# A streaming trunk of conv and attention on one core: coarser places at which attention's steps enter the projections

## The chip, the cores and the metric

The kernel runs on one core of a Trainium2 chip. The metric is the device time of one execution in microseconds (us). The kernel before takes 1231.87 us, the median of 3 runs (1231.71 to 1232.19).

The engines go by the names that the profile uses: PE is TensorE's matrix unit and PEld its weight loads, DVE is VectorE, ACT is ScalarE, POOL is GpSimd, SP is SyncE (it only issues DMAs here).

## The reference, cut to what matters

Two layers, each a SwiGLU feed-forward, a token mixer and a second SwiGLU feed-forward; layer 0 mixes by a short gated convolution, layer 1 by attention with a forget gate. There are 256 prompt frames and 64 frames of a running stream (which attends also to 256 cached frames), 320 frames in all; model width 1024, 16 heads of 64, all in float32. The part that the change touches is layer 1's mixer:

```python
def fox_project(xn, w_in, b_f, gq, gk):
    proj = xn @ w_in
    q, k, v = ...                       # 1024 columns each, 16 heads of 64
    f_logit = proj[..., 3 * D_MODEL:] + b_f
    q = rms_norm(q, gq)                 # per head
    k = rms_norm(k, gk)
    logf = jax.nn.log_sigmoid(f_logit)
    return q, k, v, logf

def fox_attend(q, k, v, c_q, c_k, q_pos, k_pos):
    s = jnp.einsum('bqhd,bkhd->bhqk', q, k) * (HEAD_DIM ** -0.5)
    decay = c_q - c_k                   # cumulative log forget, per head
    s = jnp.where(k_pos <= q_pos, s + decay, NEG_INF)
    p = jax.nn.softmax(s, axis=-1)
    return jnp.einsum('bhqk,bkhd->bqhd', p, v)

x = x + fox_attend(...) @ w_out         # prompt, and sample with its cache
```

Normalised keys, the values and the log forget gates of the new frames are outputs too.

## The kernel before, in words

**Whole program.** Seven stages follow one another: two feed-forwards around the conv mixer, the first feed-forward of layer 1, attention, the last feed-forward, with PE busy nearly all the time. Weights come in slabs, at most three at a time, each by two DMA loads on SP's queue. Every float32 weight is split into a high part (ACT casts it, L133) and a low part (DVE subtracts, L136), so that a product is three matmuls in a reduced float32 format (`mm3`, L153 to L158; high by high, high by low, low by high).

**Attention (L580 to L954).** PE's order there is not the order of the code but is made by a planner when the program is built (the loop at the end of `attn_mixer`, L927 to L954). It takes two kinds of work:

- *Dense work*, a generator, `dense()` (L878): the forget logits `pf`; then for each of two halves (eight heads) the projections of queries `pq`, keys `pk` and values `pv`, each by `project` (L847); then output projection `pm`. `project` takes its weights as two slabs, each half of the contraction (four of the eight 128-row pieces `k`), and computes three PSUM tiles `c`: two of 128 prompt frames (three matmuls for each `k`), and one for the 64 sample frames, high and low parts side by side (two matmuls for each `k`). Tiles go in the order 0, 1, 2 with the first slab and 2, 0, 1 with the second. A tile that has its second half is handed to `done`: `raw_tile` (ACT copies it out, squares it, DVE sums per head), or `value_tile`.
- *Side tasks*, a list: `gates` (L599: forget gates), `decay_tile` (per pair of heads, the mask rows: three loads per head from a DRAM copy on SP's queue, POOL adds the causal mask), `past` (loads of cached keys and values), `pair` (L746), `values_ready` (L838). There are eight pairs of heads, 0 to 3 in the first half.

A pair has four steps on PE: the *key step* (transposes of cached keys `kps` and of queries and keys `np`, from where DVE and ACT fill `ka` and `qa`, L755 to L765); the *scores* `sc` (five matmuls, L792, then `softmax`, L774 to L780, on DVE and ACT); the *transposes* `tk`, `tks` of the probabilities (L807; ACT copies them out, L810 and L813); the *output step* `oT` (L825, L830; cast to high and low by ACT L833 and DVE L834). Output projection needs a pair's result from all eight pairs; its first four tiles run over the pairs as they come.

Before each piece of dense work that `dense()` yields, the planner runs every side task whose due time has come by its own clock. That clock advances by the assumed cost of each piece, 0.2265 us (`MM`) for a projection matmul. The table `LAT` says how much later than its step a task is asked again: `norm` after the key projection (pairs 0, 2, 4, 6; two more for the odd ones), `evac` after a key step, `soft` for a softmax (counted from the end of the previous softmax where that is later), `vr` from the last value tile to the point from which a half's output steps may come. The other engines run in the order in which the code of these steps is reached, so a step that PE gets later also stands later on DVE, ACT, POOL and SP.

**Buffers.** There are four PSUM buffers for projections (`ps_mm`) and four for everything else in attention (`ps_aux`, taken by `aux(...)`): a key step takes three, scores three, transposes three, an output step one. One SBUF buffer, with the tag `ktok`, serves in turn the normalised key rows on the way out (POOL L726, then a store on SP's queue) and the 64 rows that are moved across partitions when the two halves of the sample tile are added up: `fold` (L682), a DMA on ACT's queue (L686), for queries and keys followed by DVE's add (L704), for values by POOL's. ACT issues such a DMA itself and stands until the buffer is free.

Of the kernel before, what the change touches and what calls it, by code (L numbers as in the profile page):

```python
# [30 lines left out]
KC = 8  # L31
# [3 lines left out]
SEGS = ((0, S), (S, TS))  # L35

PRE = 4
LAT = dict(rstd=2.5, gates=16, norm=8, evac=3.5, soft=5.5, pt=1, vr=1.5, out=1.8)


QT = 5
# [10 lines left out]
def trunk_kernel(  # L52
# [89 lines left out]
    def next_slab():  # L142
        if ready:
            return ready.pop(0)
        w, nk, load, split = open_slab()
        for k0 in range(0, nk, nk // 2):
            ks = slice(k0, k0 + nk // 2)
            load(ks)
            for part in split:
                part(ks)  # L150
        return w
# [428 lines left out]
    def attn_mixer(next_gain, pool):  # L580
# [9 lines left out]
        for b in range(2):  # L590
            pt = pool.tile([P, 9 * P], F32, tag=f"pt{b}", name=f"pt{b}")
# [7 lines left out]
        def gates(pf):  # L599
# [5 lines left out]
            st["RT"] = RT  # L605
            yield 0.4, LAT["rstd"]
            STT(r2T, RT, 1.0 / HD, RT, ALU.mult, ALU.mult)
# [27 lines left out]
            nc.gpsimd.dma_start(out=f_sample[0, 0], in_=lf[P - TS:P, 2])  # L635
            yield 0.8, LAT["gates"]

# [108 lines left out]
        def pair(p, n, vtok):  # L746
# [9 lines left out]
            for nj, g in zip(n, (gq, gk)):  # L756
# [5 lines left out]
                else:  # L762
                    by_tile = np_[:, :T].rearrange("p (i q) -> p i q", q=TS)
                    nc.scalar.activation(qa[b][0:HD, :, 0], by_tile[0:HD], AF.Copy, scale=g[0:HD])
                    TSC(qa[b][HD:P, :, 1], by_tile[HD:P], g[HD:P], None, ALU.mult)  # L765
            yield 0.85, LAT["evac"]
            while p not in st["rows"]:
# [14 lines left out]
        def attend(p, vpast, vtok):  # L782
# [14 lines left out]
            st["scored"][p] = 2  # L797
            st["soft"] = max(st["now"] + 1.65, st["soft"]) + LAT["soft"]
            yield 1.65, st["soft"] - st["now"] - 1.65

            kt = []
            for name, cols, heads_first in (("k0", (0, P, 2 * P, 4 * P), True), ("k1", (3 * P, 5 * P), True),
# [11 lines left out]
                kt.append(t)  # L814
            yield 1.0, LAT["pt"]
            while p not in st["v"]:
# [17 lines left out]
            TT(out=yl[:, p], in0=oT[:, :T], in1=yh[:, p].bitcast(F32), op=ALU.subtract)  # L834
            yield 1.5, LAT["out"]
            st["done"][p] = 6
# [8 lines left out]
        MM = 0.2265  # L845

        def project(name, done):  # L847


            pcs = {}  # L850
            for s in range(2):
                wh, wl = next_slab()
                wh, wl = (w.rearrange("p k c -> p (k c)").rearrange("p (k c) -> p k c", c=HW) for w in (wh, wl))
                for c in ((0, 1, 2), (2, 0, 1))[s]:
                    if s == 0:
                        pcs[c] = ps_mm.tile([P, 512], F32, tag="mm", name=name)
                    pc = pcs[c]
                    for kk in range(KC // 2):
                        k = s * (KC // 2) + kk
                        first, last = k == 0, k == KD - 1  # L860
                        if c == 2:
                            if not first:
                                nc.tensor.matmul(pc[0:TS], lhsT=xs[:, k, 0], rhs=wl[:, kk], start=False, stop=False)
                            nc.tensor.matmul(pc, lhsT=xs[:, k].rearrange("p a b -> p (a b)"), rhs=wh[:, kk],
                                             start=first, stop=last)
                            if first:
                                nc.tensor.matmul(pc[0:TS], lhsT=xs[:, k, 0], rhs=wl[:, kk], start=False, stop=False)
                            yield 2 * MM
                        else:
                            f = slice(c * P, (c + 1) * P)  # L870
                            nc.tensor.matmul(pc, lhsT=xh[:, k, f], rhs=wh[:, kk], start=first, stop=False)
                            nc.tensor.matmul(pc, lhsT=xl[:, k, f], rhs=wh[:, kk], start=False, stop=False)
                            nc.tensor.matmul(pc, lhsT=xh[:, k, f], rhs=wl[:, kk], start=False, stop=last)
                            yield 3 * MM
                    if s == 1:
                        done(c, pc)

        def dense():  # L878
            w = next_slab()
# [9 lines left out]
            for half in range(2):  # L889
                for j, name in enumerate(("pq", "pk")):  # L890
                    st["n"][j] = pool.tile([P, 3, HW], F32, tag=f"n{j}", name=f"n{j}_{half}")
                    st["m"][j] = pool.tile([P, 3, H // 2], F32, tag="qm", name=f"m{j}_{half}", bufs=2)
                    nc.gpsimd.memset(st["m"][j][TS:P, 2], 1.0)
                    yield from project(name, lambda c, pc: raw_tile(j, half, c, pc))
                    normalise(j, half)
                st["vtok"] = pool.tile([P, 3, HW], F32, tag="vtok", name=f"vtok{half}")
                for p in range(4 * half, 4 * half + 4):
                    side.append([pair(p, tuple(st["n"]), st["vtok"]), st["now"] + LAT["norm"] + 2.0 * (p % 2)])
                yield from project("pv", lambda c, pc: value_tile(half, c, pc))
                side.append([values_ready(half), 0.0])  # L900
# [63 lines left out]
    with tc.tile_pool(name="am", bufs=1) as pool:  # L964
        attn_mixer(g_ffn(1, 1), pool)
# [35 lines left out]
```

## Time and profile before

One execution was profiled; it took 1232.79 us, and the profiler's span of it is 1231.0 us.

| stretch of the span | what runs on PE | length, us | PE busy, us |
|---|---|---|---|
| 0 to 821.9 | feed-forwards and conv mixer | 821.90 | 820.75 |
| 821.9 to 928.2 | attention: logits, both halves' queries and keys, first values | 106.30 | 102.69 |
| 928.2 to 974.8 | attention: second values, first part of output projection | 46.60 | 45.92 |
| 974.8 to 992.6 | rest of output projection | 17.80 | 17.80 |
| 992.6 to 1231.0 | last feed-forward | 238.40 | 234.08 |

Instructions are named in the profile by line, engine, operation and tile (`out<-in`); L792 is line 792 of the kernel printed above. Matmuls overlap one another, so the length of one row is longer than its share of PE's time; the distance from start to start is what counts. A wait is put down to the producer that came last.

### The profile page before, as it was taken

How to read it: one execution, taken by the hardware profiler on the slowest of the kernel's cores; microseconds unless marked ns; L12 is line 12 of the kernel's file. 1: busy time of each engine (PE TensorE's matmuls, PEld its weight loads, DVE VectorE, ACT ScalarE, POOL GpSimd, SP SyncE). 2: the span in 40 equal slices, each digit the busy share in tenths (PEclk: the TensorE clock that was granted, in tenths of full speed). 3: DMA queues.
4: the chain of work that ended last, by engine and by line, in shares of the span. 5: the costliest groups of instructions: out<-in, count | busy, mean ns of one | idle time of the engine just before them, and what ended most of it. 6: DMA issues, size and time to landing. Idle time of an engine off the chain costs nothing.

```text
span 1231.0 us, 20252 instructions
## 1 busy us (share of the span) xinstructions
PE 1221.2 (99%) x8229; PEld 1188.5 (97%) x8229; DVE 764.4 (62%) x1322; ACT 493.0 (40%) x759; POOL 41.2 (3%) x95
## 2 busy tenths in 40 slices
PE   9999999999999999999999999999999999999998
PEld 9999999999999999999999999997778999999998
DVE  7665655586686655554856555467877696656432
ACT  6433433333334434333434343334555544343321
POOL 3000000000000000000000000000211000000000
PEclk9999999999999999999999999999999999999999
DMA  8644444544445444345454444354575354443451
GB/s 240 217 137 156 144 130 154 171 140 164 142 139 170 138 152 156 120 163 163 138 162 146 143 158 132 119 180 148 160 220 158 87 183 160 146 162 129 147 158 22
DMA packets 192880, 186.37 MB, mean 151 GB/s; under 512 B 17740, under 2 KB 185524, under 8 KB 192788
## 3 DMA queue, kind: packets, MB, share of 16 engines
q1 hardware_dynamic: 191552, 183.85, 47.3%
q8 instruction: 65, 1.06, 0.4%
q10 hardware_dynamic: 948, 1.16, 0.4%
q0 software_dynamic: 288, 0.08, 0.3%
q14 instruction: 27, 0.22, 0.1%
HBM read 180.26 MB, written 4.01 MB: 150 GB/s over the span
## 4 chain that ended last, share of the span: by engine, by line
PE 93%; DMA 2%; DVE 1%; ACT 1%; POOL 1%; issue 1%; SPq 0%; ACTq 0%; POOLq 0%
PE po L156 8%; PE po L158 8%; PE po L157 8%; PE pa L156 8%; PE pa L157 8%; PE pa L158 8%; PE pb L158 8%; PE pb L156 8%; PE pb L157 8%; PE pc L156 2%; PE pc L158 2%; PE pc L157 2%; PE pm L156 2%; PE pm L158 1%; PE pm L157 1%; PE head L318 1%
## 5 line engine op out<-in xcount | busy, mean ns | idle before, releaser
L136 DVE TENSOR_TENSOR wl<-wr,wh 128x1024 fp32r<-128x1024 f32 (+2 forms) x339 | 398.7, 1196 | 176.9 <-ACT wh L133 172.8
L133 ACT CAST wh<-wr 128x1024 fp32r<-128x1024 f32 (+1 forms) x334 | 332.0, 1021 | 431.3 <-issue 156.4
L158 PE MATMUL po<-gh,wl 128*128 128x320 f32 x704 | 217.0, 308 | 0.0
L156 PE MATMUL po<-gh,wh 128*128 128x320 f32 x704 | 217.0, 308 | 0.0
L157 PE MATMUL po<-gl,wh 128*128 128x320 f32 x704 | 217.0, 308 | 0.0
L156 PE MATMUL pa<-xh,wh 128*128 128x320 f32 x688 | 212.6, 309 | 0.3 <-DVE at L257 0.3
L157 PE MATMUL pa<-xl,wh 128*128 128x320 f32 x688 | 212.6, 309 | 0.0
L157 PE MATMUL pb<-xl,wh 128*128 128x320 f32 x688 | 212.5, 309 | 0.0
L158 PE MATMUL pb<-xh,wl 128*128 128x320 f32 x688 | 212.5, 309 | 0.0
L156 PE MATMUL pb<-xh,wh 128*128 128x320 f32 x688 | 212.5, 309 | 0.0
L158 PE MATMUL pa<-xh,wl 128*128 128x320 f32 x688 | 212.4, 309 | 0.0
L157 PEld LDWEIGHTS po<-gl,wh 128*128 128x128 f32 x704 | 132.1, 188 | 0.0
L158 PEld LDWEIGHTS po<-gh,wl 128*128 128x128 f32 x704 | 132.1, 188 | 0.0
L156 PEld LDWEIGHTS po<-gh,wh 128*128 128x128 f32 x704 | 132.1, 188 | 0.0
L156 PEld LDWEIGHTS pa<-xh,wh 128*128 128x128 f32 x688 | 129.2, 188 | 0.6 <-DVE at L257 0.6
L157 PEld LDWEIGHTS pa<-xl,wh 128*128 128x128 f32 x688 | 129.2, 188 | 0.0
L156 PEld LDWEIGHTS pb<-xh,wh 128*128 128x128 f32 x688 | 129.2, 188 | 0.0
L157 PEld LDWEIGHTS pb<-xl,wh 128*128 128x128 f32 x688 | 129.2, 188 | 0.0
L158 PEld LDWEIGHTS pb<-xh,wl 128*128 128x128 f32 x688 | 129.2, 188 | 0.0
L158 PEld LDWEIGHTS pa<-xh,wl 128*128 128x128 f32 x688 | 129.2, 188 | 0.0
L257 DVE TENSOR_TENSOR at<-pa,R_f 128x320 f32<-128x320 f32 x86 | 41.7, 488 | 110.8 <-PE pa L158 110.7
L466 DVE TENSOR_TENSOR bt<-pb,R_f 128x320 f32<-128x320 f32 x86 | 42.2, 491 | 59.2 <-PE pb L158 59.1
(271 smaller groups left out, 1411.8 us busy)
## 6 DMA issues: line engine op xcount, KB each, us to landing
wr<-in_ffn_w_in_dram SPq DMA_DIRECT2D x174, 512.0 KB
wr<-in_ffn_w_out_dram SPq DMA_DIRECT2D x64, 512.0 KB
wr<-in_ffn_w_out_dram SPq DMA_DIRECT2D x32, 384.0 KB
wr<-in_conv_w_in_dram SPq DMA_DIRECT2D x24, 512.0 KB
wr<-in_attn_w_in_dram SPq DMA_DIRECT2D x24, 512.0 KB
wr<-in_conv_w_out_dram SPq DMA_DIRECT2D x8, 512.0 KB
wr<-in_attn_w_out_dram SPq DMA_DIRECT2D x8, 512.0 KB
dec<-nckd SPq DMA_DIRECT2D x16, 192.0 KB
```

The lines of the kernel that those rows point to most:

```text
L133: nc.scalar.copy(out=h[:, ks], in_=r[:, ks])
L136: TT(out=l[:, ks], in0=r[:, ks], in1=h[:, ks].bitcast(F32), op=ALU.subtract)
L156: nc.tensor.matmul(ps, lhsT=wh, rhs=xh, start=first, stop=False)
L157: nc.tensor.matmul(ps, lhsT=wh, rhs=xl, start=False, stop=False)
L158: nc.tensor.matmul(ps, lhsT=wl, rhs=xh, start=False, stop=last)
L257: TT(out=at, in0=pa[:, :T], in1=R, op=ALU.mult)
L318: nc.tensor.matmul(head[m][:, :T], lhsT=w[:, k, (m % 2) * P:(m % 2 + 1) * P], rhs=x[:, k], start=(part == 0 and k == 0), stop=(part == 2 a ...
L466: TT(out=bt, in0=pb[:, :T], in1=R, op=ALU.mult)
```

## The change

Two edits.

- In `project`, the two `yield`s that stood inside the loop over `k` (after two or three matmuls) are replaced by one behind the loop, after `done`: dense work is now handed to the planner in pieces of a whole half-contraction of one tile, 12 matmuls for a prompt tile and 8 for the sample tile, with their summed cost. Side tasks can no longer enter between the pieces `k` of a tile. The forget logits and output projection still yield after every three matmuls.
- In `LAT`, `norm` goes from 8 to 10, `soft` from 5.5 to 6.2 and `vr` from 1.5 to 2.2.

```diff
-LAT = dict(rstd=2.5, gates=16, norm=8, evac=3.5, soft=5.5, pt=1, vr=1.5, out=1.8)
+LAT = dict(rstd=2.5, gates=16, norm=10, evac=3.5, soft=6.2, pt=1, vr=2.2, out=1.8)
...
                             if first:
                                 nc.tensor.matmul(pc[0:TS], lhsT=xs[:, k, 0], rhs=wl[:, kk], start=False, stop=False)
-                            yield 2 * MM
                         else:
                             f = slice(c * P, (c + 1) * P)
                             nc.tensor.matmul(pc, lhsT=xh[:, k, f], rhs=wh[:, kk], start=first, stop=False)
                             nc.tensor.matmul(pc, lhsT=xl[:, k, f], rhs=wh[:, kk], start=False, stop=False)
                             nc.tensor.matmul(pc, lhsT=xh[:, k, f], rhs=wl[:, kk], start=False, stop=last)
-                            yield 3 * MM
                     if s == 1:
                         done(c, pc)
+
+                    yield (KC // 2) * (2 if c == 2 else 3) * MM
```

Lines behind the first removed `yield` shift by one or two; up to there they stay. In the order rows the numbers behind names tell tiles of the same name apart.

The same instructions run on PE as before, in another order. In the first half's value projection, PE's order around pairs 0 and 1 was this (`kps` and `np` are key steps, `pv` the values):

```order
L864 MATMUL pv<-wh_8543,xs 128x512
L753 MATMUL kps<-ident,kpast 128x128 x2
L759 MATMUL np<-ident,n_0_8158 128x128 x3
L759 MATMUL np<-ident,n_0_8342 128x128 x3
L863 MATMUL pv<-wl_8544,xs 64x512
L864 MATMUL pv<-wh_8543,xs 128x512
L863 MATMUL pv<-wl_8544,xs 64x512
L864 MATMUL pv<-wh_8543,xs 128x512
L871 MATMUL pv<-wh_8543,xh 128x512
L872 MATMUL pv<-wh_8543,xl 128x512
L873 MATMUL pv<-wl_8544,xh 128x512
L753 MATMUL kps<-ident,kpast 128x128 x2
```

In the changed kernel the same place on PE reads:

```order
L872 MATMUL pv<-wl_8544,xh 128x512
L753 MATMUL kps<-ident,kpast 128x128 x2
L759 MATMUL np<-ident,n_0_8158 128x128 x3
L759 MATMUL np<-ident,n_0_8342 128x128 x3
L753 MATMUL kps<-ident,kpast 128x128 x2
L759 MATMUL np<-ident,n_0_8158 128x128 x3
L759 MATMUL np<-ident,n_0_8342 128x128 x3
L870 MATMUL pv<-wh_8543,xh 128x512
```

Pair 0's key step moved behind 52 of the half's value matmuls instead of 36, and pair 1's stands directly behind it, with seven value matmuls between them before.

On DVE, behind the normalising of the keys (L721, `n`), the splits of the next weight slab (L136) and the copies of pairs 0 and 1 (`ka_427` and `qa_424` are pair 0's, `ka_431` and `qa_428` pair 1's) stood like this:

```order
L721 TENSOR_TENSOR n_0_8342<-n_0_8342,y_8472 128x512 x2
L721 TENSOR_TENSOR n_0_8342<-n_0_8342,y_8472 64x512
L136 TENSOR_TENSOR wl_8904<-wr_8902,wh_8903 128x1024
L755 COPY ka_427<-kps 128x256
L765 TENSOR_SCALAR qa_424<-np,gq 64x5x64
L136 TENSOR_TENSOR wl_8904<-wr_8902,wh_8903 128x1024
L755 COPY ka_431<-kps 128x256
L765 TENSOR_SCALAR qa_428<-np,gq 64x5x64
```

In the changed kernel the same place on DVE reads:

```order
L721 TENSOR_TENSOR n_0_8342<-n_0_8342,y_8472 128x512 x2
L721 TENSOR_TENSOR n_0_8342<-n_0_8342,y_8472 64x512
L136 TENSOR_TENSOR wl_8790<-wr_8788,wh_8789 128x1024 x2
L755 COPY ka_427<-kps 128x256
L765 TENSOR_SCALAR qa_424<-np,gq 64x5x64
L755 COPY ka_431<-kps 128x256
L765 TENSOR_SCALAR qa_428<-np,gq 64x5x64
```

Both halves of a slab's split now stand ahead of pair 0's copies, and no split stands between the two pairs.

Towards the end of attention's reordered part, PE's rows from the last pair's last scores on were these (`sc` scores, `tk` and `tks` transposes, `oT` output step, `pm` output projection):

```order
L792 MATMUL sc_9659<-ka_431,qa_428 128x320
L807 MATMUL tk_9687<-ident,pt_8115 128x128 x4
L807 MATMUL tk_9694<-ident,pt_8115 128x128 x2
L807 MATMUL tks<-ident,pt_8115 128x128 x3
L156 MATMUL pm<-ayh,wh_9518 128x320
L157 MATMUL pm<-ayl,wh_9518 128x320
L158 MATMUL pm<-ayh,wl_9519 128x320
L156 MATMUL pm<-ayh,wh_9518 128x320
L157 MATMUL pm<-ayl,wh_9518 128x320
L158 MATMUL pm<-ayh,wl_9519 128x320
L825 MATMUL oT<-k_6_9692,vtok_9216 64x128 x4
```

In the changed kernel, from the same scores on:

```order
L792 MATMUL sc_9665<-ka_431,qa_428 128x320
L807 MATMUL tk_9693<-ident,pt_8115 128x128 x4
L807 MATMUL tk_9700<-ident,pt_8115 128x128 x2
L807 MATMUL tks<-ident,pt_8115 128x128 x3
L825 MATMUL oT<-k_6_9698,vtok_9212 64x128 x4
```

The six matmuls of output projection that stood between pair 6's transposes and its output step are now ahead of the scores, so that the output step follows the transposes directly.

## The prediction

> **What bounds the kernel now.** I read the page first, then the views of TensorE's (PE's) waits, of time by stretch and of PE in order of time, and last the rows of VectorE (DVE), ScalarE (ACT) and GpSimd (POOL) around the places where PE stood.
>
> ```profile
> span 1231.0 us, 20252 instructions
> ...
> PE 1221.2 (99%) x8229; PEld 1188.5 (97%) x8229; DVE 764.4 (62%) x1322; ACT 493.0 (40%) x759; POOL 41.2 (3%) x95
> ...
> PE 93%; DMA 2%; DVE 1%; ACT 1%; POOL 1%; issue 1%; SPq 0%; ACTq 0%; POOLq 0%
> ```
>
> PE is busy 99% of the span and is 93% of the chain that ended last. The change adds and removes no instruction of PE; it can only move idle time. The waits say where that lies:
>
> ```profile
> PE np L759 <- DVE n L721: 2.2, 3, 1.6
> ...
> PE tks L807 <- DVE pt L780: 0.8, 1, 0.8
> PE oT L825 <- ACT k L810: 0.7, 2, 0.5
> PE tk L807 <- DVE pt L780: 0.4, 1, 0.4
> ```
>
> All of it is in attention, in the two stretches that the change reorders:
>
> ```profile
> 821.90:928.20 106.30, 102.69 (x572) 79.24 (x570) 81.14 (x224) 56.79 (x117) 16.62 (x27) 1.00 0.63 184
> 928.20:974.80 46.60, 45.92 (x342) 39.65 (x340) 32.95 (x118) 27.36 (x74) 8.94 (x7) 1.00 0.50 141
> ```
>
> The first runs from the forget logits to the end of the second half's keys, the second from the values of that half to the point after which only output projection is left. The granted clock is 1.00 in both. Columns are length, then busy time of PE, its weight loads, DVE, ACT and POOL.
>
> **What goes.** In PE's rows (start, length) the same step stands with a wait and without:
>
> ```profile
> 866.70 0.38 PE L753 MATMUL kps<-ident,kpast 128*128 128x128 f32 x2
> ...
> 870.25 0.47 PE L863 MATMUL pv<-wl,xs 128*64 128x512 f32 x1
> ...
> 900.27 1.90 PE L792 MATMUL sc<-ka,qa 128*128 128x64 f32 x10
> ...
> 903.58 0.48 PE L871 MATMUL pq<-wh,xh 128*128 128x512 f32 x1
> ...
> 908.51 0.38 PE L807 MATMUL tk<-ident,pt 128*128 128x128 f32 x2
> ...
> 911.19 0.48 PE L871 MATMUL pq<-wh,xh 128*128 128x512 f32 x1
> ```
>
> ```profile
> 936.51 0.38 PE L753 MATMUL kps<-ident,kpast 128*128 128x128 f32 x2
> ...
> 937.36 0.47 PE L863 MATMUL pv<-wl,xs 128*64 128x512 f32 x1
> ...
> 941.36 1.90 PE L792 MATMUL sc<-ka,qa 128*128 128x64 f32 x10
> 942.86 0.63 PE L871 MATMUL pv<-wh,xh 128*128 128x512 f32 x1
> ...
> 949.22 0.82 PE L807 MATMUL tk<-ident,pt 128*128 128x128 f32 x6
> ...
> 950.12 0.39 PE L156 MATMUL pm<-ayh,wh 128*128 128x320 f32 x1
> ```
>
> (a) Pair 0's key step took 3.55 us (870.25 - 866.70), pair 4's 0.85: 2.7 lost to DVE's normalise. In the new order pair 0 comes after 52 value matmuls instead of 36, 3.7 us later (16 x 0.23), past DVE's end at 870.11 (below): **-2.7**. (b) Pair 3's scores with pair 2's transposes took 3.31; apart 1.50 + 0.90, and a lone score step hands 0.24 on to the next matmul: **-0.7**. (c) Pair 3's transposes took 2.68 instead of 0.90: **-1.8**; pair 3 now gets 28 key matmuls (6.5 us) between scores and transposes. (d) In the tail pair 4's output step waited 0.49 in its row, 0.66 from start to start; 33 projection matmuls now stand between its scores and its transposes: **-0.7**. Together **-5.9**.
>
> **What comes: first half.** (e) Pairs 0 and 1 now stand back to back. A pair takes three of the pool's four PSUM buffers, so pair 1's query transposes need the buffer that DVE's `ka` copy frees, and its key transposes the one that `qa` frees. In DVE's order the copies now stand behind both halves of a weight split, before behind one:
>
> ```profile
> 868.21 1.90 DVE L721 TENSOR_TENSOR n<-n,y 128x512 f32<-128x512 f32 x3
> 870.04 1.21 DVE L136 TENSOR_TENSOR wl<-wr,wh 128x1024 fp32r<-128x1024 f32 x1
> 871.17 0.41 DVE L755 COPY ka<-kps 128x256 f32<-128x256 f32 x1
> 871.61 0.56 DVE L765 TENSOR_SCALAR qa<-np,gq 64x320 f32<-64x320 f32 x1
> 872.20 1.85 DVE L136 TENSOR_TENSOR wl<-wr,wh 128x1024 fp32r<-128x1024 f32 x1
> ```
>
> ```profile
> 870.24 2.72 POOL L726 TENSOR_TENSOR ktok<-n,gkf 128x768 f32<-128x768 f32 x1 [1.88 <-issue]
> 875.60 1.85 POOL L726 TENSOR_TENSOR ktok<-n,gkf 128x768 f32<-128x768 f32 x1 [2.63 <-DMA out_dram<-ktok]
> ```
>
> Pair 0 starts at 870.4, pair 1's queries want their buffer at 871.5. If DVE ends its normalise at 870.1 again, the two splits end at 872.5 to 873.1, `ka` at 873.5, `qa` at 874.1: 2.2 lost. If it ends at 868.2 (the mask loads, which stood ahead of its key fold at 853 to 861, are asked for 5 us later, since the decay sums move behind 52 key matmuls), 0.2. I take **+0.9**. The first split ran 1.21 while POOL's product, begun 0.2 later, took 2.72 against 1.85; the second, begun while POOL ran, took 1.85. [...]
>
> (f) Pairs 4 and 5, the same way, with DVE done at 937.2 and the pair at 940.3: **+0.3** (0 to 1.0). (g) A pair step directly behind transposes (pairs 2 and 6) waits for ACT's copies out of the buffers; scores followed by a pair step cost 0.2 more than apart: **+0.4** for both (0 to 0.8). (h) Pair 2's transposes stand behind pair 3's key step and need buffers freed by `ka` and `qa` of pair 3. On DVE these follow a weight split whose cast may begin only when the second half's query contraction is over (its buffer): 4.5 us after pair 2's scores begin, plus cast 1.05, two splits 2.45, `ka` 0.4, a reduction 0.7 and `qa` 0.6 make 9.9, against 9.0 where PE arrives: **+1.0** (0.3 to 1.5).
>
> (i) Query norms and pair 3's softmax now stand behind DVE's L704, which waits for a DMA that folds half a tile:
>
> ```profile
> 836.89 0.50 ACTq L686 DMA_DIRECT2D part<-n  x1
> ```
>
> ```profile
> 839.81 0.68 DVE L704 TENSOR_TENSOR n<-n,part 64x512 f32<-64x512 f32 x1
> ```
>
> ```profile
> 901.59 0.48 ACTq L686 DMA_DIRECT2D part<-n  x1
> ```
>
> ```profile
> 908.33 0.68 DVE L704 TENSOR_TENSOR n<-n,part 64x512 f32<-64x512 f32 x1 [4.15 <-DMA part<-n]
> ```
>
> The same fold was usable 2.9 us after its issue once and 6.7 the other time. It is issued some 8 us after pair 2's scores. At 2.9 nothing is lost. At 6.7 ACT's square of the folded tile holds up pair 2's last two copies, so its output step waits up to 2.9, and DVE starts pair 3's softmax so late that its transposes wait up to 2.5. I take 4.5 us: 0.7 + 0.9 = **+1.6** (0 to 5). [...]
>
> **What comes: tail.** (j) After pair 4's output step only six projection matmuls are free (0.9 us) before those that need its result; ACT's and DVE's casts take 1.3 to 2.2 after the step: **+0.7** (0.1 to 1.2). (k) Pair 7's key step is followed by nine matmuls (1.3 us) instead of 24 (3.6) before its scores:
>
> ```profile
> 962.34 0.38 PE L753 MATMUL kps<-ident,kpast 128*128 128x128 f32 x2
> ```
>
> ```profile
> 964.61 0.56 DVE L765 TENSOR_SCALAR qa<-np,gq 64x320 f32<-64x320 f32 x1
> ```
>
> Its `qa` ended 2.8 us after the step began, with pair 6's softmax on DVE between; PE now arrives after 2.2, and DVE's order has two more softmax operations (0.35 + 0.25) ahead: **+0.9** (0.2 to 2). (l) Behind the last scores the two last pairs' exponentials and copies on ACT set the pace:
>
> ```profile
> 966.95 1.90 PE L792 MATMUL sc<-ka,qa 128*128 128x64 f32 x10
> ...
> 969.69 0.40 PE L156 MATMUL pm<-ayh,wh 128*128 128x320 f32 x1
> ...
> 974.79 0.41 PE L156 MATMUL pm<-ayh,wh 128*128 128x320 f32 x1
> ```
>
> Those 7.84 us also held six projection matmuls; the new order has them earlier, and the stretch stays as long: **+0.9**.
>
> **Sum.** -5.9 + 0.9 + 0.3 + 0.4 + 1.0 + 1.6 + 0.7 + 0.9 + 0.9 = **+0.8 us**. Whole half-contractions save nothing by themselves: behind transposes and key steps the next two matmuls start no later than undisturbed ones (937.36 follows the last transpose at its own pace). The moved DMAs cost nothing directly: the mask loads now behind the value fold's store on SP's queue have some 7 us until the scores of pairs 2 and 3, and 2 until pair 7's. The profiled execution took 1232.79 (span 1231.0, 1.8 around it), 0.9 over the median of 1231.87; on the median the forecast is 1231.9 + 0.8 = **1232.7 us**.
>
> **Rivals.** Slower: ACT's fold of the values.
>
> ```profile
> 947.31 0.47 ACTq L686 DMA_DIRECT2D partv<-vtok  x1
> 947.83 0.35 ACT L776 ACTIVATE pt<-pt,st 128x64 f32<-128x64 f32 x1 [2.05 <-DVE pt L780]
> ```
>
> It may not be issued until the last key rows have been written out (its buffer is theirs), and ACT stands: here until 19.1 us after the values began (928.2). Now a cast, a value copy and all ten exponentials of pairs 4 and 5 stand behind it. Up to 18.5 PE does not notice; from there each microsecond is one on PE at pair 4's transposes, and part of it again at (j). At 20.5, with 0.5 more at (j), it is +2.5: **1235.2**. Against it: the normalise that feeds the key rows may end earlier. Faster: no new queue forms. Then (e), (f), (g), (h) and (i) fall to 0.2, 0, 0, 0.3 and 0 and the tail to 0.1 + 0.2 + 0.9, 1.7 in all, and -4.2 is left: **1227.7**; half of that way, at 1230, is where such a run would more likely lie. For it: DVE is idle for a quarter of the time. Against it: (h) and (l) follow from the orders alone. No effect at all (the steps not moved) would be 1231.9, but the orders differ.
>
> **How the numbers follow.** Net near nothing (forecast): 0.60; slow fold or several bounds high: 0.28; faster: 0.12. A measurement can tell 0.2%, 2.5 us, from no change, so faster 0.12, same 0.60, slower 0.28. The ends of (e) and (i) reach furthest up, so the range is 1229.0 to 1236.5.
>
> **What would show it.** Right: no wait of np for n; the largest waits in front of pair 1's np, pair 2's tks, pair 7's sc; first stretch some 1.5 us shorter, second some 2.3 longer (the sums of the terms by stretch). Wrong: PE waiting for softmax in the tail by more than 1 us (the slower rival), no waits at pairs 1 and 2 (the faster one), or a longer time behind 974.8, where nothing should change.

## The result, and the profile after

The changed kernel takes 1240.44 us (median of 6 runs, 1240.01 to 1243.18) against 1232.16 (1231.71 to 1234.42) of the kernel before in the same set: a ratio of 1.0067, interval 1.0057 to 1.0077. It is slower by 8.3 us; the forecast was 1232.7 with a range up to 1236.5, so both the size and the range were wrong. Profiled, the changed kernel took 1240.01 and the kernel before 1232.79, so the two traces differ by 7.2.

The page of the changed kernel, with the rows that answer to those of before (share of the span and number of instructions behind each engine's busy time):

```profile
span 1237.8 us, 20253 instructions
...
PE 1222.8 (99%) x8229; PEld 1189.6 (96%) x8229; DVE 760.7 (61%) x1322; ACT 492.9 (40%) x759; POOL 40.8 (3%) x95
```

PE has the same 8229 instructions and about the same busy time; the span is 6.8 us longer. Its waits (engine, line, whom it waited for, us in total, times, longest) and the same stretches as before, cut at the same places of the program (forget logits, second half's values, last output tiles; columns as in the prediction):

```profile
PE tks L807 <- DVE qa L765: 6.8, 1, 6.8
PE oT L825 <- ACT k L810: 1.3, 4, 0.6
...
PE sc L792 <- DVE qa L765: 0.8, 1, 0.8
...
PE kps L753 <- DVE ayl L834: 0.2, 1, 0.2
```

```profile
821.30:933.20 111.90, 104.25 (x572) 80.85 (x569) 77.53 (x224) 57.63 (x117) 17.02 (x25) 0.95 0.61 169
933.20:981.60 48.40, 46.51 (x343) 39.82 (x340) 33.02 (x119) 26.72 (x74) 8.17 (x9) 1.00 0.50 148
981.60:999.40 17.80, 17.80 (x124) 17.66 (x121) 15.66 (x32) 9.08 (x14) 0.00 (x0) 1.00 0.18 60
```

The first stretch grew from 106.3 to 111.9 us (+5.6, where -1.5 was forecast), the second from 46.6 to 48.4 (+1.8, where +2.3 was forecast); behind them nothing changed, and the part ahead of them, which the change does not touch, took 0.6 us less (821.3 instead of 821.9). The many small waits of before are gone, np for n among them. One wait of 6.8 us has come, and in the first stretch the granted clock is no longer 1.00. PE's rows around it, in order of time (start, length; in brackets the idle time ahead and who ended it), and then the clock (the column behind POOL) in three pieces:

```profile
904.31 0.38 PE L753 MATMUL kps<-ident,kpast 128*128 128x128 f32 x2
904.52 0.82 PE L759 MATMUL np<-ident,n 128*128 128x128 f32 x6
905.18 0.82 PE L807 MATMUL tk<-ident,pt 128*128 128x128 f32 x6
912.82 0.90 PE L807 MATMUL tks<-ident,pt 128*128 128x128 f32 x3 [6.82 <-DVE qa L765]
913.38 0.78 PE L870 MATMUL pk<-wh,xh 128*128 128x512 f32 x1
...
918.74 0.88 PE L825 MATMUL oT<-k,vtok 128*64 128x128 f32 x12
```

```profile
907.00:908.40 1.40, 0.00 (x0) 0.00 (x0) 0.00 (x0) 0.00 (x0) 0.00 (x0) 1.00 1.08 194
908.40:918.60 10.20, 5.78 (x15) 4.34 (x15) 4.26 (x11) 4.19 (x9) 1.00 (x2) 0.50 0.54 151
918.60:920.00 1.40, 1.40 (x26) 1.20 (x26) 1.17 (x7) 0.00 (x0) 0.00 (x0) 0.99 0.00 0
```

Behind pair 3's key step PE does pair 2's first six transposes and then stands for 6.8 us, because the last three need a PSUM buffer that pair 3's `qa` frees. The clock is granted at half from 908.4, 2.4 us after the last matmul's end at 906.0, until 918.6. The next 12 key matmuls take 918.74 - 913.38 = 5.36 us instead of 12 x 0.233 = 2.80: another 2.6. Those 9.4 us are more than the whole loss between the two traces.

Why `qa` was so late stands on ACT:

```profile
905.05 1.07 ACT L693 COPY n<-pq 128x512 f32<-128x512 f32 x2 [1.58 <-PE np L759]
910.07 0.53 ACTq L686 DMA_DIRECT2D part<-n  x1
910.64 0.60 ACT L705 ACTIVATE pq<-n 128x512 f32<-128x512 f32 x1 [4.52 <-DMA dec<-nckd]
911.18 0.58 ACT L693 COPY n<-pq 128x512 f32<-128x512 f32 x1
911.66 0.52 ACT L764 ACTIVATE qa<-np,gq 64x320 f32<-64x320 f32 x1
```

```profile
915.35 0.68 DVE L704 TENSOR_TENSOR n<-n,part 64x512 f32<-64x512 f32 x1 [2.58 <-DMA part<-n]
```

ACT copies the second half's query tiles into `n` only when pair 3's key step has read the old `n` (the 1.58 us for np). In the kernel before, that key step stood ahead of the end of these tiles, and ACT had pair 3's `qa` behind it before the first copy into `n`:

```profile
895.70 1.03 PE L759 MATMUL np<-ident,n 128*128 128x128 f32 x6
```

```profile
896.74 0.51 ACT L764 ACTIVATE qa<-np,gq 64x320 f32<-64x320 f32 x1
...
899.08 0.59 ACT L693 COPY n<-pq 128x512 f32<-128x512 f32 x1
```

ACT's order is not simply the order in which the code is reached, as the description of the kernel has it: in the changed kernel the sample query tile's last matmul started at 890.31, ahead of pair 2's scores, and its copy (the first of the two at 905.05) stands behind pair 2's exponentials and two weight casts.

With the copies done, ACT comes to the fold L686, is ready for it at 906.12 and issues it at 910.07; the profile puts that wait on the next row, as one for a mask load, `dec`. In the trace each DMA names a completion semaphore, on which counts come in as it lands. In this program the DMAs of SP and ACT take eight of them in turn (the trace numbers them 100, 102 and 104 to 109), and in the profiles of both kernels none of these DMAs, 501 in each, was issued before the last one on its semaphore had all its counts, most of them 16. For the fold that was the first mask load of pair 4, on 108 as well, whose counts came from 907.12 to 909.97:

```profile
900.86 1.07 SPq L660 DMA_DIRECT2D dec<-nckd  x1
```

Only behind this stand of 3.9 us does ACT reach `qa`.

### The profile page after: what moved, and what is told of

It reads as the page before. It is cut to its first block, busy times and chain, and to the rows that moved or that the text cites. A ratio compares the mean times of both kernels' runs of the same rounds, so it can differ in the third digit from the quotient of the medians.

```text
span 1237.8 us, 20253 instructions
## 1 busy us (share of the span) xinstructions
PE 1222.8 (99%) x8229; PEld 1189.6 (96%) x8229; DVE 760.7 (61%) x1322; ACT 492.9 (40%) x759; POOL 40.8 (3%) x95
## 3 DMA queue, kind: packets, MB, share of 16 engines
q1 hardware_dynamic: 191552, 183.85, 46.6%
q8 instruction: 65, 1.06, 0.4%
## 4 chain that ended last, share of the span: by engine, by line
PE 96%; DVE 1%; ACT 1%; DMA 1%; issue 0%; ACTq 0%; DVEq 0%
PE po L158 8%; PE po L156 8%; PE po L157 8%; PE pa L156 8%; PE pa L157 8%; PE pa L158 8%; PE pb L157 8%; PE pb L156 8%; PE pb L158 8%; PE pc L156 2%; PE pc L157 2%; PE pc L158 2%; PE pm L156 2%; PE pm L158 1%; PE pm L157 1%; PE head L318 1%
## 5 line engine op out<-in xcount | busy, mean ns | idle before, releaser
L136 DVE TENSOR_TENSOR wl<-wr,wh 128x1024 fp32r<-128x1024 f32 (+2 forms) x339 | 396.7, 1191 | 174.2 <-ACT wh L133 170.4
```

The lines of the kernel that those rows point to most:

```text
L136: TT(out=l[:, ks], in0=r[:, ks], in1=h[:, ks].bitcast(F32), op=ALU.subtract)
```

## The experiments

All kernels ran next to the kernel before; ratios are to that kernel in the same set.

### Each edit alone, and the fold on other queues

The theory at this point, S: ACT's stand for the semaphore is the loss.

```diff
lat_only:    LAT of the change, the old yields
coarse_only: the new yields, old LAT
fold_sp, fold_pool (on the changed kernel):
-            nc.scalar.dma_start(out=part, in_=t[TS:P])
+            nc.sync.dma_start(out=part, in_=t[TS:P])       # fold_sp
+            nc.gpsimd.dma_start(out=part, in_=t[TS:P])     # fold_pool
```

> Only the three LAT entries of the change; projections still yield after each k. Theory S (a shared completion semaphore): in the changed kernel the second half's query fold (a DMA on ACT's queue) could not be issued until the DMA that had used its completion semaphore before it, the first mask load of pair 4, had landed; ACT stood from 906.1 to 910.1, pair 3's query copy behind it came late, PE waited 6.8 us for the PSUM buffer and then ran 12 matmuls at half clock (2.6 us). Here the fold follows a slab load on its semaphore that was asked for earlier, so S expects no such stall: 1231 to 1234 us. Rival L (the later LAT times alone cost): 1236 or more. Rival Y (coarse pieces cost, LAT does not): 1231 to 1233.

> Only the coarse yields of the change; LAT as before. Theory S: the fold here follows a load of cached values on its semaphore, landed before it is wanted; no wait over 1 us at tks, clock 1.00 throughout, 1230 to 1233 us. Rival Y (steps packed between whole half-contractions wait for one another): most of the loss is here, 1237 to 1241. Rival B (pair 3's key step straight ahead of pair 2's transposes takes the PSUM buffers they need): no loss here either, since 24 matmuls stand between them in this order, so this run does not part B from S.

> The changed kernel with the folds issued on SP's queue instead of ACT's; PE's order is the same row for row. Theory S: the fold still waits for its semaphore, but ACT does not stand behind it; pair 3's query copy goes ahead, the wait at tks falls from 6.8 to 1 to 3 us, little or no half clock: 1231 to 1236 us. Rival B (PSUM buffers and the order on PE): tks still waits 5 us or more, 1238 to 1241.

> The changed kernel with the folds issued on POOL's queue, whose DMAs have completion semaphores of their own; PE's order is the same row for row. Theory S: neither ACT nor the fold waits for a mask load; the wait at tks falls to 1 to 3 us, clock 1.00: 1230 to 1235 us, the rest above 1230 being what POOL's slower issue costs. Rival B: tks still waits 5 us or more, 1238 to 1241. Rival D (the burst of weight and mask loads makes every DMA late, whichever queue): the fold is usable no earlier than 915, as in the changed kernel (915.3), and PE waits behind it.

Measured: lat_only 1245.07 (ratio 1.0103, 1.0087 to 1.0119), coarse_only 1242.56 (1.0078, 1.0065 to 1.0090), fold_sp 1241.61 (1.0070, 1.0058 to 1.0083), fold_pool 1240.97 (1.0065, 1.0052 to 1.0079). LAT alone is slower than both edits together, the coarse yields alone are no faster (the two intervals overlap); of the expectations only L's "1236 or more" has room for that. Taking the DMA off ACT gains nothing in time. S is not enough. The largest waits of PE in the four, one fence each in this order:

```profile
PE oT L825 <- ACT k L810: 4.6, 5, 2.0
PE tk L807 <- DVE st L774: 4.4, 1, 4.4
```

```profile
PE oT L825 <- ACT k L810: 5.0, 5, 3.4
PE sc L792 <- ACT k L810: 4.7, 1, 4.7
```

```profile
PE tk L807 <- DVE pt L780: 5.1, 2, 3.1
PE tks L807 <- ACT ka L761: 2.5, 1, 2.5
```

```profile
PE tks L807 <- ACT ka L761: 2.3, 1, 2.3
PE np L759 <- DVE st L774: 1.9, 1, 1.9
PE tks L807 <- DVE pt L780: 1.5, 1, 1.5
```

At tks the wait did fall from 6.8 to 2.5 and 2.3, as S said and against rival B, but each kernel lost the time at another step: pair 3's transposes behind a softmax, its scores behind copies on ACT. What stands ahead of those, among the second half's queries, is the same in all: DVE's add L704, which waits for the fold. It is not the whole loss: the longest waits at output steps (oT) in lat_only (2.0) and coarse_only (3.4) stand behind a fold of values on ACT, and fold_pool's 1.9 is pair 7's key step behind a softmax that waits for late mask rows. In fold_pool POOL issued the fold at 905.87, in 0.53 us like ACT in the changed kernel, with semaphores of its own (111 to 118 for POOL's DMAs in the changed kernel's trace), and in lat_only ACT at 903.76, and still it was usable only at

```profile
912.35 0.69 DVE L704 TENSOR_TENSOR n<-n,part 64x512 f32<-64x512 f32 x1 [4.22 <-DMA part<-n]
```

```profile
910.90 0.68 DVE L704 TENSOR_TENSOR n<-n,part 64x512 f32<-64x512 f32 x1 [5.07 <-DMA part<-n]
```

6.5 and 7.1 us after its issue. Rival D, which had the fold usable no earlier than 915 on any queue, is wrong about the time and right that the other queue does not make the fold quick. In coarse_only ACT's fold waited, by the profile, 2.7 us for another DMA, a load of cached values. So the theory became F: the fold's whole way, from wanted to usable, and DVE's and ACT's in-order queues behind it.

### Without the folds

These kernels leave the low rows of the sample tile out of queries and keys; the fold of the values stays.

```diff
                 if c == 2:
-                    TT(out=n[0:TS, 2], in0=n[0:TS, 2], in1=part, op=ALU.add)
...
-                st["part"] = (fold(n[:, 2], f"{j}{half}"), pc)
+                st["part"] = (None, pc)
```

> The changed kernel without the query and key folds: the rows 64 to 127 of each sample tile (the low part of its activations times the weights) are not moved and not added; the values keep theirs. PE's order is the same row for row. Theory F (formed after the first four runs, each of which lost at another step behind the same DMA): the second half's query fold takes 6 to 9 us from wanted to usable, DVE's add and ACT's square stand for it in their order, and whatever step of pairs 2 and 3 is queued behind them makes PE wait. F expects the wait at tks to fall from 6.8 to about 3 us (ACT's three copies and three squares still stand ahead of pair 3's query copy, since the copies need pair 3's key step), no other wait over 1.1 us, clock 1.00 or one short spell at half: 1232 to 1235 us. Rival B (the key step ahead of the transposes alone): 1238 or more.

> The kernel before without the query and key folds (same part left out). F: the fold cost the kernel before only 1.8 us, at pair 3's transposes (the wait put down to DVE's softmax, which stood behind the add): 1230 to 1232 us. Rival B expects the same here.

> Coarse yields with LAT as before, without the query and key folds (same part left out). F: of the loss with the folds (waits of 4.7 us at pair 3's scores for ACT's copies, which stood behind the square of the folded tile, and a spell at half clock) nothing is left in the first half; the tail's loss (3.4 us at pair 4's output step behind ACT's value fold, and half clock) stays, since that fold stays: 1234 to 1238 us. Rival Y (coarse pieces cost by themselves): as with the folds, 1241 to 1243.

> The three LAT entries alone, without the query and key folds (same part left out). F: the wait of 4.4 us at pair 3's transposes (behind DVE's add) and the second spell at half clock go; what stays are the waits of pair 0 behind ACT's value fold in the first half (about 3 us and a spell at half clock) and pair 4's in the tail (2 us and more): 1236 to 1241 us. Rival L (the LAT times cost by themselves): as with the folds, 1244 to 1246.

| base | with the folds | without | ratio without, interval |
|---|---|---|---|
| before | 1232.86 | 1231.91 | 0.9990 (0.9981 to 0.9999) |
| changed | 1240.44 | 1235.59 | 1.0022 (1.0013 to 1.0031) |
| coarse yields alone | 1242.56 | 1231.70 | 0.9988 (0.9979 to 0.9997) |
| LAT alone | 1245.07 | 1235.12 | 1.0018 (1.0010 to 1.0027) |

Each ratio is to the kernel before of its own set. The folds cost the kernel before 1 us, the changed one 4.8 (5.5 by the two ratios), and each edit alone 10 to 11. F holds. nofold_a ended 0.6 us above its range, with the wait and the spell at half clock that were expected. For coarse yields and for LAT alone the expectations were too high. In coarse_only I expected the value fold's loss in the tail to stay; PE's wait at pair 4's output step fell from 3.4 us with a spell at half clock to 1.3 without one. Rival Y falls: coarse pieces without folds cost nothing. Of rival L some 3 us are left (1.0018 against 0.9990): the largest waits of nofold_lat are 1.97 and 1.35 us at the output steps of pairs 0 and 4, behind the value fold that these kernels keep.

But nofold_a still takes 3 us more than the kernel before. Its waits and the rows of ACT at that place:

```profile
PE tks L805 <- ACT ka L759: 3.0, 1, 3.0
```

```profile
905.26 1.56 ACT L693 COPY n<-pq 128x512 f32<-128x512 f32 x3 [1.58 <-PE np L757]
906.70 1.64 ACT L703 ACTIVATE pq<-n 128x512 f32<-128x512 f32 x3
908.27 0.52 ACT L762 ACTIVATE qa<-np,gq 64x320 f32<-64x320 f32 x1
```

Three query tiles wait for pair 3's key step; then their copies and squares, 3.0 us, stand ahead of pair 3's own `qa`.

### What is left: ACT's order, or the late key step

```diff
nofold_hp, pefold_hp_a: the copies to qa and ka (L761 to L765) under tc.high_priority()
pefold_*:
                 if c == 2:
-                    st["part"] = (fold(n[:, 2], f"{j}{half}"), pc)
+                    low = pool.tile([P, HW], BF16, tag="low", name=f"low{j}{half}")
+                    nc.scalar.copy(out=low, in_=pc)
...
+                        if c == 1 and name != "pv":        # behind the last tile's matmuls
+                            part = aux("part")[0:TS]
+                            nc.tensor.matmul(part, lhsT=shift, rhs=low, start=True, stop=True)
...
-            nc.scalar.dma_start(out=part, in_=t[TS:P])     # now the values' fold only
+            nc.sync.dma_start(out=part, in_=t[TS:P])
```

> The changed kernel without the query and key folds (same part left out as there), and with a pair's query and key copies out of PSUM given priority over other work that is ready on ACT and DVE. Theory N: the 3.0 us that PE still waits at pair 2's transposes, and the 1.7 us lost to the half clock behind it, come from ACT's order: the query tiles' three copies need the single buffer n, which pair 3's key step frees, and they and their squares stand ahead of pair 3's own query copy. With that copy first, N expects the wait at tks below 1 us and no spell at half clock: 4 us less, 1230 to 1233 us. Rival B (three PSUM buffers taken by the key step, whatever ACT does first): the wait stays above 2 us, 1234 to 1237.

> The changed kernel with the same outputs but without the DMA: the low rows are copied to a bf16 tile by ACT, moved to rows 0 to 63 by one matmul of PE with a shifted identity (512 columns, after the last tile's matmuls) and added by DVE from PSUM; the value fold goes to SP's queue; the copies have the priority of the run above. F and N together expect the loss gone: four matmuls of 0.23 us are added, 1230 to 1233 us. If something else in the change costs, 1235 or more.

> Coarse yields with LAT as before, folds of queries and keys by PE as above, the value fold on SP's queue. Against the same kernel without folds (1231.7): ACT no longer stands for the value fold, which cost 1.7 + 1.9 us around pair 0's output step and 1.3 + 1.5 around pair 4's; four matmuls are added (0.9 us), and the fourth PSUM buffer is held for some microseconds: 1227.5 to 1231 us. If a new queue forms on SP behind the value fold: 1232 or more.

> The kernel before with the folds of queries and keys by PE and the value fold on SP's queue. Against the same kernel without folds (1231.9): the 2.2 + 2.4 us around pair 0's output step and 0.4 + 0.5 around pair 4's go, four matmuls come (0.9 us): 1228 to 1231 us; 1232 or more if the held PSUM buffer or SP's queue costs as much.

nofold_hp took 1234.35 (1.0014, 1.0005 to 1.0023), not 1230 to 1233; that is rival B's range, but not by B's mechanism. The wait at tks is gone, as theory N said, with the two steps still back to back; but another came at the next key tile, which needs a projection buffer that a query tile still holds:

```profile
PE pk L869 <- DVE m L704: 2.1, 1, 2.1
```

So N names a symptom: whatever goes first on ACT, three tiles' copies and squares begin only after pair 3's key step. pefold_hp_a (1235.64; 1.0023, 1.0014 to 1.0031) shows the same wait, 1.9 us, and missed its 1230 to 1233. pefold_sp_c took 1235.73 (1.0024, 1.0014 to 1.0034) and missed as well: ACT's waits went, but SP stood 1.7 us for the value fold, and PE waited 3.2 us for cached keys queued behind it and eleven mask loads, the new queue that its expectation named. What share of the 3.2 us is the fold's was not tried.

pefold_sp_b, the kernel before with these folds, took **1230.52 us, ratio 0.9982 (0.9974 to 0.9991)**: within its 1228 to 1231, and 0.2% faster than the kernel before. No wait over 0.3 us is left in its attention:

```profile
PE sc L795 <- DVE ka L758: 0.3, 1, 0.3
...
PE oT L828 <- ACT k L813: 0.2, 1, 0.2
```

### The key step moved

```diff
nofold_earlyk_a, earlyk_a: kpast loaded when pair p - 2 is scored, vpast when it is done;
  a pair's key step waits for kpast only
early_a, nofold_early_a:
+            st["past"][p] = (kpast, vpast)
             yield 0.0, 0.0
-            st["past"][p] = (kpast, vpast)
```

> The changed kernel without the query and key folds (same part left out), with the key steps of pairs 2, 3, 6 and 7 placed right behind the scores of pairs 0, 1, 4 and 5: the cached keys are loaded as soon as the pair two before is scored, the cached values when it is done. Theory K: n is free before the second half's first query tile is done; no wait at tks and none of pk for DVE's sums: 1229 to 1232 us. Rival P: 1234 or more, as without this move (1235.6).

> The same with the folds in place. Theory F with K: the fold is wanted some 5 us earlier, but still among the weight and mask loads; what it holds up is what DVE and ACT have queued behind it, softmax and copies of pairs 2 and 3: 1 to 6 us more than without folds, 1231 to 1237. If the changed kernel's whole loss hung on the late key step: no more than 0.5 us above the run without folds.

> The changed kernel, folds in place, with one statement moved: a pair's cached rows count as loaded when the loads are issued, not one piece of dense work later. Pair 3's key step comes 12 matmuls (2.8 us) earlier, pair 2's transposes 12 matmuls after it. K and F: the wait at tks goes, since pair 3's copies have 2.8 us; the fold is issued about 2 us earlier, and what is left is a wait behind it at pair 3's scores or transposes: 1233 to 1238 us. Rival P: 1239 to 1241.

The first two were a bad instrument: 1243.31 (1.0081, 1.0067 to 1.0095) and 1245.57 (1.0101, 1.0087 to 1.0115). Two scores and two key steps in a row ask for more than the four buffers of `ps_aux`, and PE stood for softmax to free them, up to 2.9 us at a time, and for copies of `ka`, up to 3.1:

```profile
PE np L756 <- DVE st L771: 5.8, 3, 2.9
PE np L756 <- DVE ka L752: 5.2, 2, 3.1
```

That is what packing costs when it is overdone, and it hides what the totals were to show. early_a took 1239.58 (1.0057, 1.0043 to 1.0071), above my 1233 to 1238 and in the range of rival P (1239 to 1241). The waits still went as K and F said: the one at tks fell from 6.8 to 1.0, and a new one of 3.4 came at pair 3's scores, for copies on ACT behind the folded tile's square. With the fold in place, time saved ahead of it is lost behind it. The last three runs settle the rest.

```diff
nomask_a (on the changed kernel), in decay_tile:
+            if p >= 4:
+                st["rows"][p] = st["rows"][p - 2]
+                return
pefold_early_a: early_a with the folds of pefold_sp_b
```

> early_a without the query and key folds (same part left out): coarse pieces and LAT of the change, pair 3's key step 12 matmuls earlier, and those 12 now stand between it and pair 2's transposes. Theory K: neither tks (3.0 us without this move) nor pk waits for the late copies, no spell at half clock in the first half; what is left are waits of about 1.5 us in all at pair 0's and pair 6's steps: 1231 to 1233 us. Rival P (packing as such): 1235 to 1236, as without the move.

> The changed kernel with its folds, but without the mask loads of pairs 4 to 7, which use the mask rows of the pair two before; the order on PE and on ACT is the same row for row. Theory F: the fold follows an earlier weight load on its completion semaphore and is issued at 906 to 907 instead of 910.1; with fewer loads in front of it it is usable at 909 to 912 instead of 915.3; the wait at tks falls from 6.8 to 3 to 4 us: 1235 to 1238 us. Rival (the mask loads are not what delays it): issued at 910, 1239 to 1241.

> early_a (coarse pieces and LAT of the change, cached rows counted as loaded when issued) with the folds of queries and keys by PE and DVE and the value fold on SP's queue; same outputs. Theories F and K: no wait above 1 us before the last two pairs, clock 1.00; against the same kernel without folds (1231.8) the value fold's waits go (1 us) and four matmuls come (0.9): 1230 to 1232.5 us, so at or a little behind the kernel before with the same folds (1230.5), since the change has no gain left but the waits that the folds caused. If coarse pieces have a gain of their own: below 1230.

nofold_early_a took **1231.77, ratio 0.9991 (0.9982 to 1.0000)**: one piece of 12 matmuls between the two steps, and the changed kernel without folds is as fast as the kernel before without them (0.9990). K, by which the late key step is what costs, holds, and P, by which the packing as such costs, falls. (This move also parts the two steps. That being back to back is not what costs at tks, nofold_hp has shown: there they stand back to back and tks does not wait.) nomask_a took 1234.44 (1.0011, 1.0002 to 1.0020), a little below the range:

```profile
906.16 0.47 ACTq L689 DMA_DIRECT2D part<-n  x1
...
912.90 0.60 ACT L708 ACTIVATE pq<-n 64x512 f32<-64x512 f32 x1 [3.29 <-DVE n L707]
```

Without those loads the fold is issued at 906.16, as soon as ACT comes to it, and DVE adds it at 912.18 instead of 915.35; the wait at tks falls to 2.4. So the mask loads held up the issue by 3.9 us. The way itself still took 6.0, with the weight loads in front of it; that these alone make it slow was not tried. pefold_early_a took 1232.73 (0.9997, 0.9988 to 1.0007), 0.2 us above its range: with the key step, the folds of queries and keys and the value fold repaired, the change is level with the kernel before and behind pefold_sp_b. No gain of its own is seen.

## Why the prediction was wrong

**Bound and place: right.** PE is the bound, behind attention nothing changed, the order on PE is the one shown, and no np waits for n.

**What goes, (a) to (d): right.** All four waits are gone; (a) to (c) promised -5.2 in the first stretch.

**(e), (f), (g): small.** The two back-to-back key steps cost 0.2 each in their rows of PE (2.06 us for both pairs), the low ends of (e) and (f). What went unpriced is pair 0's output step: ACT stood for the value fold in the first half, the mechanism of the slower rival in another place. It is worth about 1.0: PE's rows lost 0.3 us at that pair's last transposes, 0.45 at its output step and 0.45 in front of the key step behind it, of which 0.2 are (g).

**(h) failed: +1.0 (0.3 to 1.5) was forecast.** I had seen the place, pair 2's transposes behind pair 3's key step, and took DVE's splits for what delays `qa` (its terms add up to 9.7, not 9.9, so by its own sum to 0.7). It was ACT. The step left out that `n` has one buffer: the query tiles' copies are held until that same key step and then run ahead of `qa`. That alone is 3.0 us in nofold_a, and 1.7 for the half clock behind it (12 matmuls in 4.45, from 909.62 to 914.07, instead of 2.80): 4.7 together; a single piece between the two steps undoes it (nofold_early_a).

**(i) failed: +1.6 (0 to 5).** The mechanism was right, in-order queues standing behind the fold, and what leaving the folds out saved, 4.8 us, lies within its bounds; the 1.6 was a third of it. Two things in it were wrong. The fold's cost was counted from its issue (2.9 to 6.7 us), as if ACT could always issue it; it waited 3.9 us for a mask load's landing first, and was usable 9.2 us after ACT was ready. And the cost was laid on the output step and on softmax, where some cover was left; the 3.9 us fell on pair 3's `qa`, ahead of transposes with none, and so added to (h) (6.8 instead of 3.0 at tks) instead of standing beside it. From its issue the fold took 5.3 us on ACT's queue (910.07 to 915.35) and 6.5 on POOL's (905.87 to 912.35).

**No step had a price for the half clock.** 2.6 of the 9.4 us are matmuls at half speed. Terms (h) and (i) together were put at 2.6 and measured 9.4; that difference of 6.8, plus about 1.0 for pair 0 and less 0.7 from (e), is the 7.1 by which the first stretch missed.

**The tail: right in the sum.** +2.3 forecast, +1.8 measured; (j) cost about nothing instead of 0.7, (k) 0.8 at pair 7's scores, and (l) is there: the last steps take as long as before (7.9 us) without the six projection matmuls among them.

**Rivals.** The slower rival had the right kind of cause, ACT standing at a fold that may not be issued, but its place, the tail's value fold, cost nothing here (issued at 950.3, 17.1 after the values began, under its 18.5). The faster rival is not borne out: nofold_early_a, in whose attention no wait but two, of 0.6 and 0.4 us, is over 0.3, took 1231.77, not 1227.7 to 1230. The terms of a packed place were priced one by one and summed; together they were one wait with no cover at all.

## What to carry to other kernels

Where a step is moved, list what its operands' buffers hold back, on other engines too: here a key step moved later on PE kept three tiles from being copied, and their work then stood ahead of the step's own result. The small DMA that ACT issued between two pieces of arithmetic had two waits, in the changed kernel 3.9 us for its semaphore and 5.3 for its landing, with many loads around it; a matmul with a shifted identity, with a copy of 0.59 us on ACT ahead of it, did the same move for 0.34 us of PE, from its start to the next (pefold_sp_b, 908.72 to 909.06). And when each of several variants loses at a different step, look for what they queue behind in common, before mending the step that the profile names.

## What the runs showed of the hardware

**Two stops of PE cost more than their length.** Behind the 6.8 us stop of the changed kernel the next 12 matmuls took 2.6 us more than at full clock, behind the 3.0 us stop of nofold_a 1.7. Half clock (0.50) came in spells of 3.4, 6.8 and 10.2 us: 3.4 behind the stop of nofold_a (909.5 to 912.9), 6.8 in lat_only (912.4 to 919.2), 10.2 around the stop of the changed kernel (908.4 to 918.6). These are one, two and three times 3.4; what sets the length was not tried. A shorter stop was followed by a spell in one run and not in another: at pair 0's output step PE stood 2.0 us both in lat_only and in nofold_lat, and only lat_only has the half clock behind it (888.5 to 891.9); the mean clock of nofold_lat's profile is 1.000.

**The fold took 2.3 us at a DMA share of 0.34 and 3.9 to 7.4 at 0.82 to 1.08.** The same fold of 64 rows by 512, from its issue (L686) to the start of the addition that waits for it (L704), beside the mean busy share of the 16 DMA engines over that time:

| run and place | issued at | usable after, us | DMA share |
|---|---|---|---|
| changed kernel, first half's queries | 835.81 | 2.3 | 0.34 |
| fold_sp, second half's queries (this and below) | 911.76 | 3.9 | 0.84 |
| changed kernel | 910.07 | 5.3 | 0.82 |
| nomask_a | 906.16 | 6.0 | 0.94 |
| fold_pool | 905.87 | 6.5 | 0.94 |
| before | 901.59 | 6.7 | 0.87 |
| lat_only | 903.76 | 7.1 | 1.06 |
| coarse_only | 902.85 | 7.4 | 1.08 |

That the load is the cause was not tried apart.
